# mLSTM heads in units of half the tokens, with a unit's outputs emitted behind the next unit's weights

## The chip, the core and the metric

The kernel runs on one core of one Trainium2 chip. Of the core's engines five matter here: TensorE (PE in the rows; its weight loads are PEld), VectorE (DVE), ScalarE (ACT), GpSimd (POOL) and SyncE (SP), which only issues transfers. The metric is the device time of one execution in microseconds, lower is better.

## What is computed

A two-layer bidirectional encoder on 1024 tokens of width 1024. Each layer mixes tokens with four groups of heads side by side (mLSTM, pooling windows, differential attention, grouped-query attention), then attends to a memory of 256 tokens, then runs a gated convolutional feed-forward net. The change touches the first part, the mLSTM heads above all:

```python
def mlstm_chunkwise(q, k, v, li, lf):        # per head; run forwards and, flipped, backwards
    b = cumsum(lf); a = g - b + li           # gates of a chunk
    C_loc = einsum('l,ld,le->de', exp(a - max(a)), k, v)   # what a chunk adds to the state
    ...                                      # scan over chunks: C_prev, n_prev, m_prev
    wts = exp(dlog - m_t) * einsum('td,sd->ts', q, k)      # weights inside a chunk
    num = einsum('ts,sd->td', wts, v) + exp(e - m_t) * einsum('td,de->te', q, C_prev)
    den = sum(wts) + exp(e - m_t) * einsum('td,d->t', q, n_prev)
    return num / maximum(abs(den), exp(-m_t))
```

There are 4 such heads of 64 channels in a layer, each in both directions.

## The kernel before

**Stages of a layer's mixing.** First `tok_pass` projects what is needed token by token. Then `mix` (from L1096) fills three queues of Python generators. Queue 0 holds the 15 dense projections (`qk_steps`, `ml_project`, `pool_steps`), each 48 matmuls of 512 columns (L353, L355, L357: high and low parts of both operands) into a two-bank `sc` tile. Queue 1 holds the mLSTM (`ml_gates`, then `ml_steps`). Queue 2 holds the chains behind the projections (`qk_chain`: group sums, rotation, scaling). A loop pumps them in turn: each pass hands 1 credit to queue 0, 0.6 to queue 1 and 1.0 to queue 2, and a generator says at each `yield` how many credits its step was worth. I call this the **projection stretch**. After it the attention heads run (`attend`: grouped-query first, L685 to L688, then differential, L634), and what is left in the queues is pumped behind them in small doses, along with dense work on the memory tokens (`memory_keys`, 192 matmuls of 256 columns in a layer; `memory_values`, L1381 to L1383) and the output projection.

**What sets the order.** The instructions are emitted in the order of the pumping, and a list scheduler then places them on each engine when their operands and buffers are free in its model; each engine runs its list in that order. Buffers come from pools: `work` (17 tiles named `t`), `small` (8 named `s`), `evac` (2 named `e`), and in PSUM `tp` (3 banks), `fl` (1 bank) and `sc` (2 double banks). In the built order tiles of one pool are first written in the order in which they were asked for.

**PSUM of the mLSTM.** `ml_()` gives one of the three `tp` banks while `self.wide` is set, that is, in the projection stretch, and the single `fl` bank afterwards. `memory_keys` takes the same `fl` bank once and holds it over all its 192 matmuls.

**One head** (`ml_head`): loads V, K, Q; 8 transposes of K (L947); weighted keys (DVE, L950); chunk states in two banks (L959; ACT copies L964, L965); the scan over chunks (DVE, L968). Then for each half of the tokens (I call this a **unit**): scaled queries (PE L975, DVE L977); for both directions the exponents (PE L982 and L983, ACT L988); scores (PE L996) and their product with the weights (DVE L1000); and for both directions the outputs: 8 matmuls a direction, 65 columns each (L1009 with the weights, L1012 with the state; one fewer L1012 at a sequence end), followed by the division (DVE L1017 to L1028, POOL L1029). A float32 matmul of this kind stands as two in the trace. The outputs of a unit are emitted directly behind its weights, eight matmuls between two yields of 1.5:

```python
            nc.vector.tensor_tensor(out=wt, in0=wt, in1=st.unsqueeze(1)..., op=ALU.mult)   # L1000
            yield 1.5
            for d in range(2):
                po = self.ml_()
                for c in range(4): ...                                                     # L1009, L1012
```

`ml_project` (L781) makes the mLSTM's q, k and gate projections. Its evacuation writes each half from `sc` into a tile of the two-buffer pool `evac` (L788 or L790) and stores it to DRAM by SP, from where `ml_head` loads it.

## Time and profile before

| | us |
|---|---|
| median of 3 runs | 3496.82 (3492.69 to 3504.57) |
| the profiled execution | 3500.49 |
| its span, first to last instruction | 3498.7 |
| PE busy in the span | 3302.9 (94%) |
| DVE, ACT, POOL busy | 2102.3 (60%), 1439.2 (41%), 681.8 (19%) |
| projection stretch, layer 0 and 1 | about 140 to 385 and 1890 to 2113 |
| grouped-query attention, layer 0 and 1 | about 385 to 600 and 2113 to 2330 |

In the timeline and window rows, times count from the span's start. "PEclk" is the mean granted TensorE clock of a stretch as a share of 2.4 GHz; the chip grants 2.4 GHz or 1.2 GHz (0.50), so a mean between them tells which share of the stretch ran at which. A busy PE at 0.50 is busy for twice the time.

### The profile page before, as it was taken

To read this page: it belongs to the slowest core of one execution; us is meant where nothing else is said; L and a number is where in the kernel's file an instruction comes from. 1 tells how busy PE (TensorE), PEld (TensorE's weight loads), DVE (VectorE), ACT (ScalarE), POOL (GpSimd) and SP (SyncE) were. 2 spreads that over 40 slices of the span, in tenths; PEclk is the share of its full clock that TensorE was granted. 3 is DMA by queue.
4 is the path that set the end of the run, shared out by engine and by line. 5 is a ranking of instruction groups with operands and counts; after the bars stand their busy time and mean duration, and the time that the engine had idled before them with its cause. 6 is when DMAs were issued, how large, how long until landed. Compare 5 with 4: busy or idle time off the path is not lost.

```text
span 3498.7 us, 43627 instructions
## 1 busy us (share of the span) xinstructions
PE 3302.9 (94%) x16782; PEld 2762.6 (79%) x16782; DVE 2102.3 (60%) x3266; ACT 1439.2 (41%) x2411; POOL 681.8 (19%) x484
## 2 busy tenths in 40 slices
PE   7999988999999999999999898899898999999999
PEld 7877777987777888778897777789777878887787
DVE  4445667875456777753435356778735577777432
ACT  4222556753444444431323235577535344434211
POOL 2110435842110000000112004467411100000000
PEclk9988889999999999999999888999999999999999
DMA  5343335423242222255543433344214312222654
GB/s 181 98 127 108 108 92 161 146 75 109 84 144 74 85 79 85 79 189 192 179 130 107 136 96 120 102 157 139 105 61 137 122 61 85 78 85 79 203 189 155
DMA packets 156197, 414.57 MB, mean 118 GB/s; under 512 B 31251, under 2 KB 49301, under 8 KB 155989
## 3 DMA queue, kind: packets, MB, share of 16 engines
q1 hardware_dynamic: 136372, 380.32, 33.0%
q10 hardware_dynamic: 19616, 31.46, 2.8%
q8 instruction: 132, 2.16, 0.3%
q14 instruction: 77, 0.62, 0.1%
HBM read 276.19 MB, written 128.19 MB: 116 GB/s over the span
## 4 chain that ended last, share of the span: by engine, by line
PE 77%; DVE 11%; DMA 6%; ACT 3%; issue 3%; POOL 1%; SPq 0%; ACTq 0%; DVEq 0%; POOLq 0%
PE sc L1681 15%; PE sc L353 11%; PE sc L355 11%; PE sc L357 11%; PE tp L1681 6%; DVE smax L479 2%; PE tp L537 2%; DMA raw<-w_ffn_in 1%; DVE s L542 1%; DMA yd<-s 1%; PE sc L634 1%; PE tp L1009 1%; PE tp L276 1%; PE tp L528 1%; PE tp L1012 1%
## 5 line engine op out<-in xcount | busy, mean ns | idle before, releaser
L328 ACT CAST wp<-raw 128x1024 fp32r<-128x1024 f32 (+2 forms) x174 | 165.4, 952 | 579.8 <-PE sc L355 469.0
L353 PE MATMUL sc<-h,wp 128*128 128x512 f32 x1120 | 361.1, 402 | 18.8 <-DVE e L790 9.6
L357 PE MATMUL sc<-h,wp 128*128 128x512 f32 x1120 | 359.5, 401 | 13.0 <-DVE wp L329 13.0
L355 PE MATMUL sc<-h,wp 128*128 128x512 f32 x1120 | 362.4, 402 | 0.0
L1681 PE MATMUL sc<-h,wp 128*128 128x512 f32 x1320 | 338.4, 397 | 10.7 <-DVE t L1691 7.5
L1681 PE MATMUL sc<-t,wp 128*128 128x512 f32 x1320 | 328.3, 394 | 7.3 <-DVE t L1569 4.1
L1681 PEld LDWEIGHTS sc<-h,wp 128*128 128x128 f32 x1320 | 246.8, 190 | 75.7 <-DVE t L1691 20.7
L1681 PEld LDWEIGHTS sc<-t,wp 128*128 128x128 f32 x1320 | 251.2, 191 | 61.3 <-DVE t L1569 4.7
L244 POOL TENSOR_TENSOR rb<-rb,z 128x1024 f32<-128x1024 f32 x34 | 92.2, 2712 | 901.6 <-ACT z L243 833.6
L353 PEld LDWEIGHTS sc<-h,wp 128*128 128x128 f32 x1120 | 212.8, 193 | 67.9 <-DVE e L790 10.0
L357 PEld LDWEIGHTS sc<-h,wp 128*128 128x128 f32 x1120 | 214.9, 193 | 62.6 <-DVE wp L329 15.2
L479 DVE TENSOR_REDUCE smax<-sc 128x1 f32<-128x1024 f32 x192 | 233.3, 1217 | 43.3 <-PE sc L688 24.2
L355 PEld LDWEIGHTS sc<-h,wp 128*128 128x128 f32 x1120 | 215.5, 193 | 48.8 <-issue 3.5
L482 ACT ACTIVATE h<-sc,smax 128x1024 f32<-128x1024 f32 x192 | 214.8, 1120 | 70.6 <-DVE smax L479 51.8
L1568 ACT CAST wp<-s 128x512 fp32r<-128x512 f32 x176 | 109.2, 623 | 318.6 <-PE sc L1681 296.3
L1289 DVE TENSOR_TENSOR z<-sc,z 128x1024 f32<-128x1024 f32 x64 | 78.3, 1223 | 254.5 <-PE sc L357 254.4
L353 PE MATMUL sc<-t,wp 128*128 128x512 f32 x640 | 201.1, 395 | 12.8 <-ACT wp L328 10.0
L542 DVE TENSOR_TENSOR s<-tp,s 128x512 fp32r<-128x512 f32 x256 | 172.9, 683 | 65.4 <-ACT s L541 64.2
L1681 PE MATMUL tp<-h,wp 128*128 128x512 f32 x792 | 202.0, 390 | 2.3 <-ACT wp L1568 2.3
L355 PE MATMUL sc<-t,wp 128*128 128x512 f32 x640 | 200.6, 395 | 2.4 <-DVE t L1258 2.4
L357 PE MATMUL sc<-t,wp 128*128 128x512 f32 x640 | 198.9, 392 | 0.0
L537 PE MATMUL tp<-identr,h 128*128 128x128 f32 x1024 | 183.1, 284 | 15.3 <-DVE s L542 11.7
(426 smaller groups left out, 7215.0 us busy)
## 6 DMA issues: line engine op xcount, KB each, us to landing
raw<-w_ffn_in SPq DMA_DIRECT2D x88, 512.0 KB
xd<-z SPq DMA_DIRECT2D x72, 512.0 KB
z<-xd SPq DMA_DIRECT2D x72, 512.0 KB
gd<-t SPq DMA_DIRECT2D x44, 512.0 KB
z<-gd SPq DMA_DIRECT2D x44, 512.0 KB
raw<-w_ffn_out SPq DMA_DIRECT2D x32, 512.0 KB
raw<-w_fm SPq DMA_DIRECT2D x30, 512.0 KB
raw<-w_ck SPq DMA_DIRECT2D x16, 512.0 KB
```

Of the source, the lines that this page charges most:

```text
L244: nc.gpsimd.tensor_tensor(out=st["acc"], in0=st["acc"], in1=sq, op=ALU.add)
L328: nc.scalar.copy(hi, raw)
L353: nc.tensor.matmul(o, lhsT=hi[:, k, :], rhs=xh[:, f : f + m], start=first, stop=False)
L355: nc.tensor.matmul(o, lhsT=hi[:, k, :], rhs=xl[:, f : f + m], start=False, stop=False)
L357: nc.tensor.matmul(o, lhsT=lo[:, k, :], rhs=xh[:, f : f + m], start=False, stop=last)
L479: nc.vector.tensor_reduce(out=m, in_=sc, axis=AX.X, op=ALU.max, negate=True)
L482: nc.scalar.activation(e, sc, AF.Exp, bias=m, scale=1.0, accum_out=s)
L537: nc.tensor.transpose(tp[:, (2 * j + i) * P : (2 * j + i + 1) * P], w[:, (k + j) * P : (k + j + 1) * P], self.ident)
L542: nc.vector.tensor_tensor(out=el, in0=tp, in1=eh.bitcast(F32), op=ALU.subtract)
L1289: nc.vector.tensor_tensor(out=x, in0=ps, in1=x, op=ALU.add)
L1568: nc.scalar.copy(hi, x)
L1681: mm = lambda a, b, start, stop: nc.tensor.matmul(ps, lhsT=a, rhs=b, start=start, stop=stop, skip_group_check=not first)
```

## The change

1. **Units.** `ml_head` is split into `ml_state` (loads, K transposes, states), `ml_weights` (one unit up to L1000's product) and `ml_outputs` (that unit's outputs). `ml_steps` emits a unit's outputs behind the weights of the following unit; across heads they come before the next head's state. The outputs are cut into pieces: a yield of 0.4 after each chunk's matmuls.
2. **More waiting credits.** 3 credits pass between a head's loads and its transposes, 3 more before the states.
3. **Buffers.** The scaled queries and the second direction's product go to `small` tiles instead of a `work` tile; `ml_project` evacuates into `small` instead of `evac`.
4. **Pace.** Queue 1 gets 0.7 credits a pass instead of 0.6. `qk_chain` yields between the two halves of its group sums (L276) and asks for 2 credits more in all.

```diff
@@ qk_chain
         pg = self.tp_()
+        yield 2
         for h in range(2):
             self.group_sums(pg, G, 4 * G * h, sq[h], ind, nt=4)
+            yield 1
         y = self.group_rsqrt(pg, G, dim, r[1], times=times)
-        yield 3
+        yield 1
@@ ml_project
-            t = self.e_()
+            t = self.s_()
@@ ml_state (the first part of ml_head)
             nc.sync.dma_start(out=Q[p : p + 64], in_=self.MQ[f, p0 : p0 + 64])
+        yield 3
...
-        yield 1
+        yield 3
...
+                if c == 1:
+                    yield 0.4
...
-            yield 1
+            yield 0.4
@@ ml_weights
+        WT, QS = self.t_(), self.s_()
...
-            yield 0.5
+        yield 0.4
...
-                yield 1
+            yield 0.6
...
-            yield 1.5
+        out.append((wt, QS))
+        yield 0.6
@@ ml_outputs
+                if c < 3:
+                    yield 0.4
...
-                    t = QT[:, HF : HF + 256].rearrange("p (c e) -> p c e", e=64)
+                t = self.s_()[:, :256].rearrange("p (c e) -> p c e", e=64)
...
-                yield 1.5
+            yield 0.4
@@ ml_steps
+        behind = None
         for h in range(4):
             for gen in needs[h // 2]:
                 self.until(gen)
-            yield from self.ml_head(l, h, g, HT)
+            state = []
+            if behind:
+                yield 3
+                yield from self.ml_outputs(*behind)
+                behind = None
+            yield from self.ml_state(l, h, g, state)
+            for n in range(2):
+                made = []
+                yield from self.ml_weights(l, h, n, g, state[0], made)
+                if behind:
+                    yield from self.ml_outputs(*behind)
+                behind = l, h, n, g, state[0], made[0], HT
+        yield 4
+        yield from self.ml_outputs(*behind)
@@ mix
-            self.pump(0.6, 1)
+            self.pump(0.7, 1)
```

**How it moves instructions.** Three places of layer 0; layer 1 is alike. In the names the number behind a tile is its count; lines of the changed kernel are shifted (L947 is L950 there, L959 L962, L975 L986, L982 and L983 L992 and L993, L996 L1006, L1009 and L1012 L1026 and L1029, L1000 L1010, L537 L539, L541 L543, L685 L687).

Place 1, PE where the third head begins. Before, the last outputs of the second head run into the group sums and into the third head's transposes and states:

```order
L1009 MATMUL tp_2048<-t_1685,t_1773 128x65
L1012 MATMUL tp_2048<-t_1685,t_1774 128x65
L1009 MATMUL tp_2048<-t_1685,t_1773 128x65
L276 MATMUL tp_2083<-cons,s_1951 128x4 x4
L276 MATMUL tp_2083<-cons,s_1952 128x4 x4
L947 MATMUL tp_2178<-identr,t_2172 128x64 x8
L959 MATMUL tp_2189<-t_2169,t_2177 128x65 x4
L959 MATMUL tp_2211<-t_2169,t_2177 128x65 x4
L975 MATMUL tp_2232<-t_1003,mltab 128x512
L982 MATMUL tp_2235<-t_993,mltab 128x512
```

In the changed kernel the third head's transposes stand between dense matmuls:

```order
L357 MATMUL sc_2243<-h_187,wp_2235 128x512 x2
L353 MATMUL sc_2243<-h_195,wp_2234 128x512
L950 MATMUL tp_2266<-identr,t_2204 128x64 x8
L308 MATMUL tp_2289<-identr,gy_332_2215 4x128 x4
L308 MATMUL tp_2299<-identr,gy_332_2215 4x128 x4
L353 MATMUL sc_2243<-h_195,wp_2234 128x512
L355 MATMUL sc_2243<-h_196,wp_2234 128x512 x2
```

What moved: the last outputs and the next head's start no longer form one row of small matmuls. The outputs of a unit themselves still stand as 14 or 15 of a row in both kernels.

Place 2, PE around a unit's scores. Before, the outputs of the unit whose scores these are follow at once:

```order
L982 MATMUL tp_1976<-t_993,mltab 128x512
L983 MATMUL tp_1976<-mltab,identr 128x512
L996 MATMUL tp_2000<-t_1690,t_1688 128x128 x4
L1009 MATMUL tp_2018<-t_1685,t_1773 128x65
L1012 MATMUL tp_2018<-t_1685,t_1774 128x65
```

In the changed kernel the outputs behind the scores read the weights of the unit before (t_2351, not the product of tp_2442):

```order
L355 MATMUL sc_2536<-h_188,wp_2531 128x512 x2
L357 MATMUL sc_2536<-h_187,wp_2532 128x512 x2
L353 MATMUL sc_2536<-h_195,wp_2531 128x512 x2
L687 MATMUL sc_2711<-t_1621,t_1629 128x512
L1006 MATMUL tp_2442<-t_2206,t_2204 128x128 x4
L1026 MATMUL tp_2472<-t_2201,t_2351 128x65 x2
L1029 MATMUL tp_2472<-t_2201,s_2352 128x65
```

What moved: a unit's outputs no longer follow its own scores.

Place 3, ACT in the grouped-query attention, where the memory keys end. L328 makes the high part of a weight, L1365 to L1370 (L1331 to L1336 before) evacuate the memory keys' `fl` bank, L541 (L543) makes attention operands. Before, attention's casts stand between those of the memory keys:

```order
L541 CAST s_3056<-tp_3051 128x512
L328 CAST wp_3699<-raw_3698 128x1024
L1331 COPY z_2847<-fl_2850 128x256
L1336 ACTIVATE e_3446<-fl_2850 128x256
L541 CAST s_3074<-tp_3069 128x512
L541 CAST s_3109<-tp_3104 128x512
L328 CAST wp_3961<-raw_3960 128x1024
```

In the changed kernel the last head's states, in `fl`, and its scaled queries come first:

```order
L328 CAST wp_5012<-raw_5011 128x1024
L1365 COPY z_2775<-fl_2777 128x256
L1370 ACTIVATE e_4718<-fl_2777 128x256
L969 COPY t_2656<-fl_2900 64x260
L970 COPY t_2656<-fl_2900 64x3x65
L969 COPY t_2656<-fl_2952 64x195
L970 COPY t_2656<-fl_2952 64x4x65
L543 CAST s_3001<-tp_2996 128x512
```

On PE at the same place the last 125 memory-key matmuls stand in a row and then this:

```order
L357 MATMUL fl_2777<-h_2740,wp_4582 128x256
L950 MATMUL fl_2803<-identr,t_2659 128x64 x8
L962 MATMUL fl_2900<-t_2656,t_2802 128x65 x4
L962 MATMUL fl_2952<-t_2656,t_2802 128x65 x4
L986 MATMUL fl_2993<-t_994,mltab 128x512
L529 MATMUL tp_2976<-s_3001,t_1627 128x256
```

What moved: before, only the fourth head's last unit (and one direction of the unit before it) lies in the `fl` bank, behind the memory keys; now the fourth head's states and both its units do, and ACT makes no attention operand between the cast of the keys' fourth weight and the end of that head's states. From the end of the memory keys to the start of `memory_values` (the next dense matmuls of this stretch) PE's list transposes attention weights of 13 blocks of 128 queries before (from the 10th to the 23rd) and of 21 now (from the 4th to the 25th).

## Rows read from the trace of the kernel before

**Rows 1.** Cores: span and mean granted TensorE clock.

```profile
core 0: 3498.7 us, clock 0.957
```

**Rows 2.** Windows: stretch, length, busy time (instructions) of PE, PEld, DVE, ACT, POOL; PEclk; DMA.

```profile
140.00:385.00 245.00, 233.34 (x1059) 185.28 (x1057) 126.67 (x245) 70.92 (x139) 36.77 (x32) 0.87 0.39 120
...
465.00:535.00 70.00, 60.65 (x342) 51.29 (x341) 54.76 (x104) 41.40 (x80) 30.60 (x21) 0.87 0.29 91
...
605.00:745.00 140.00, 135.71 (x1038) 127.25 (x1037) 126.73 (x212) 102.45 (x181) 106.56 (x84) 1.00 0.36 123
...
1890.00:2113.00 223.00, 210.05 (x957) 165.71 (x955) 114.39 (x228) 66.97 (x132) 31.07 (x28) 0.87 0.37 113
```

**Rows 3.** Waits of PE in layer 0's projection stretch: total us, times, longest.

```profile
PE sc L353 <- DVE e L790: 4.3, 1, 4.3
PE tp L947 <- DMA t<-mkd: 1.8, 1, 1.8
```

**Rows 4.** The same of layer 1.

```profile
PE sc L353 <- DVE e L790: 5.4, 1, 5.4
PE tp L947 <- DMA t<-mkd: 3.1, 1, 3.1
```

**Rows 5.** Line L1000: who waited for it (us, times), both layers.

```profile
  PE tp L1009: 5.1, 4
```

**Rows 6.** Timeline of DVE, layer 0: start, length, instruction, idle before and its releaser.

```profile
225.19 0.69 DVE L790 SCALAR_TENSOR_TENSOR e<-sc,rb 128x512 f32<-128x512 f32 x1 [10.11 <-DMA mkd<-e]
```

**Rows 7.** Timeline of PE, layer 0, two runs of small matmuls.

```profile
272.86 0.44 PE L1009 MATMUL tp<-t,t 128*128 128x65 f32 x2
273.23 0.43 PE L1012 MATMUL tp<-t,t 64*128 64x65 f32 x2
...
302.54 0.69 PE L1009 MATMUL tp<-t,t 128*128 128x65 f32 x2
303.15 0.69 PE L1012 MATMUL tp<-t,t 64*128 64x65 f32 x2
...
312.63 1.11 PE L947 MATMUL tp<-identr,t 64*128 64x64 f32 x8
315.43 3.65 PE L959 MATMUL tp<-t,t 128*128 128x65 f32 x16 [1.69 <-DVE ry L216]
```

**Rows 8.** Windows of the longest stretch at the lower clock in each layer.

```profile
301.10:321.60 20.50, 18.82 (x76) 16.21 (x76) 6.89 (x28) 2.48 (x9) 0.72 (x1) 0.50 0.30 72
2041.90:2062.40 20.50, 18.82 (x77) 15.89 (x76) 7.40 (x29) 3.62 (x11) 0.72 (x1) 0.50 0.25 60
```

**Rows 9.** Timeline of ACT in the attention of layer 0 and of layer 1.

```profile
447.50 0.59 ACT L541 CAST s<-tp 128x512 fp32r<-128x512 f32 x1 [10.52 <-DMA yd<-s]
...
2183.61 0.59 ACT L541 CAST s<-tp 128x512 fp32r<-128x512 f32 x1 [8.73 <-DMA yd<-s]
```

**Rows 10.** Waits of PE from 385 to 605, and from 2113 to 2335.

```profile
PE tp L527 <- DVE s L542: 11.1, 4, 8.0
...
PE tp L527 <- DVE s L542: 9.1, 3, 6.2
```

**Rows 11.** Windows, L537's transposes alone (PE, PEld; eight for 128 queries).

```profile
465.00:535.00 70.00, 19.95 (x107) 14.25 (x106) 0.87 0.29 91
```

**Rows 12.** Groups by line from 385 to 605: count, busy us, mean ns, idle before.

```profile
L329 POOL TENSOR_TENSOR wp<-raw,wp 128x1024 fp32r<-128x1024 f32 x14 | 33.4, 2391 | 23.1 <-ACT wp L328 23.1
L328 ACT CAST wp<-raw 128x1024 fp32r<-128x1024 f32 x14 | 14.6, 1053 | 16.3 <-issue 6.5 <-PE fl L355 3.9 <-PE fl L1382 2.8
...
L964 ACT COPY t<-tp 64x195 f32<-64x195 f32 x1 | 0.3, 302 | 0.0
```

**Rows 13.** Timeline of PE: two neighbouring matmuls of the memory keys.

```profile
432.63 0.28 PE L353 MATMUL fl<-h,wp 128*128 128x256 f32 x1
432.74 0.28 PE L355 MATMUL fl<-h,wp 128*128 128x256 f32 x1
```

**Rows 14.** Line L950: duration min/median/max in ns.

```profile
L950 DVE TENSOR_TENSOR t<-tp,mtok x16: 679/682/692, 160.1 to 2118.6; 128x512 f32<-128x512 f32 x16
```

More of the change, by code (lines that the diff above doesn't have):

```diff
@@ L927, in ml_gates, with ml_state @@
         out.append((pairs, tok, fb))
-    def ml_head(self, l, h, g, HT):
+    def ml_state(self, l, h, g, out):
         nc = self.nc
-        (mt, si), tok, fb = g[0]
+        _, tok, fb = g[0]
         f, p0 = h // 2, (h % 2) * 64
-        hf = lambda: self.t_()
-        vc = hf()
+        vc = self.t_()
         V = vc[:, : 8 * 65].rearrange("p (c e) -> p c e", e=65)
@@ L938, in ml_head @@
         nc.gpsimd.memset(V[:, :, 64:65], 1.0)
-        K = hf()[:64]
+        K = self.t_()[:64]
         nc.sync.dma_start(out=K, in_=self.MK[f, p0 : p0 + 64])
-        Q = hf()
+        Q = self.t_()
         for p in (0, 64):
             nc.sync.dma_start(out=Q[p : p + 64], in_=self.MQ[f, p0 : p0 + 64])
-        KW = hf().rearrange("p (c d e) -> p c d e", d=2, e=64)
+        yield 3
+        KW = self.t_().rearrange("p (c d e) -> p c d e", d=2, e=64)
         pk = self.ml_()
@@ new lines, in ml_state, with ml_weights @@
+        out.append((V, C, K, Q))
+    def ml_weights(self, l, h, n, g, state, out):
+        nc = self.nc
+        (mt, si), tok, _ = g[0]
+        _, _, K, Q = state
+        sl = slice(n * HF, (n + 1) * HF)
+        WT, QS = self.t_(), self.s_()
+        pi = self.ml_()
+        nc.tensor.matmul(pi, lhsT=self.ml_sel(h)[:100], rhs=si[:100, sl], start=True, stop=True)
+        nc.vector.tensor_tensor(out=QS, in0=Q[:, sl], in1=pi, op=ALU.mult)
+        yield 0.4
+        for d in range(2):
+            pm = self.ml_()
+            one = self.mltab[:100, h * P + 64 * d : h * P + 64 * d + 1].to_broadcast([100, P])
+            nc.tensor.matmul(pm, lhsT=one, rhs=mt[:100, sl], start=True, stop=False)
+            nc.tensor.matmul(
+                pm, lhsT=self.identr, rhs=self.mltab[:, (4 + d) * P : (5 + d) * P].unsqueeze(1).to_broadcast([P, 4, P]),
+                start=False, stop=True,
+            )
+            for c in range(4):
+                nc.scalar.activation(
+                    WT[:, d * HF + c * P : d * HF + (c + 1) * P], pm[:, c * P : (c + 1) * P], AF.Exp,
+                    bias=tok[:, 0, d, 4 * n + c, h : h + 1], scale=-1.0,
+                )
+            yield 0.6
+        st = self.ml_()
+        for c in range(4):
+            o = (4 * n + c) * P
+            nc.tensor.matmul(
+                st[:, c * P : (c + 1) * P], lhsT=K[:, o : o + P], rhs=Q[:64, o : o + P], start=True, stop=True
+            )
+        wt = WT.rearrange("p (d n) -> p d n", d=2)
+        nc.vector.tensor_tensor(out=wt, in0=wt, in1=st.unsqueeze(1).to_broadcast([P, 2, HF]), op=ALU.mult)
+        out.append((wt, QS))
+        yield 0.6
@@ new lines, in ml_outputs @@
+    def ml_outputs(self, l, h, n, g, state, made, HT):
+        nc = self.nc
+        tok = g[0][1]
+        V, C, _, _ = state
+        wt, QS = made
+        for d in range(2):
+            po = self.ml_()
+            for c in range(4):
+                cc = 4 * n + c
+                prev = cc - 1 if d == 0 else cc + 1
+                inter = 0 <= prev < 8
+                out = po[:, c * 65 : (c + 1) * 65]
+                nc.tensor.matmul(out, lhsT=wt[:, d, c * P : (c + 1) * P], rhs=V[:, cc, :], start=True, stop=not inter)
+                if inter:
+                    q = slice(64 * d, 64 * d + 64)
+                    nc.tensor.matmul(
+                        out, lhsT=QS[q, c * P : (c + 1) * P], rhs=C[q, prev if d == 0 else 7 - prev, :], start=False, stop=True
+                    )
+                if c < 3:
+                    yield 0.4
+            ov = po[:, :260].rearrange("p (c e) -> p c e", e=65)
+            den = self.tiny(4, tag="mden", bufs=3)
+            nc.vector.tensor_reduce(
+                out=den, in_=ov[:, :, 64:65], axis=AX.X, op=ALU.max, apply_absolute_value=True
+            )
+            nc.vector.tensor_tensor(out=den, in0=den, in1=tok[:, 2, d, 4 * n : 4 * n + 4, h], op=ALU.max)
+            nc.vector.reciprocal(den, den)
+            db = den.unsqueeze(2).to_broadcast([P, 4, 64])
+            dst = HT[n][:, :, h, :]
+            if d == 0:
+                nc.vector.tensor_tensor(out=dst, in0=ov[:, :, 0:64], in1=db, op=ALU.mult)
+            else:
+                t = self.s_()[:, :256].rearrange("p (c e) -> p c e", e=64)
+                nc.vector.tensor_tensor(out=t, in0=ov[:, :, 0:64], in1=db, op=ALU.mult)
+                nc.gpsimd.tensor_tensor(out=dst, in0=dst, in1=t, op=ALU.add)
+            yield 0.4
```

53 lines of the change are left out of this document (removed).

## The prediction

> **What bounds the kernel now.** I read the span and the clock first. The core runs 3498.7 us at a mean granted clock of 0.957 [rows 1], and PE is busy for most of every stretch, so a change gains only where PE idles or is granted 1.2 GHz, and moves nothing by shifting work between other engines. The windows by stage say where that is. In the projection stretch PE is busy 233.3 of 245 us in layer 0 and 210.1 of 223 in layer 1, and its clock is 0.87 in both [rows 2]. In the first part of the attention, once the memory keys are through, it is busy 60.7 of 70 us, again at 0.87, while in the differential attention it is busy 135.7 of 140 at 1.00 [rows 2]. So there are three pools to gain from or lose to: PE's waits in the projection stretch, its slow clock there, and the poorly filled stretch of attention. The waits by releaser, the timeline around the longest slow stretches, and the attention's stalls then give the terms below. All sums are over both layers.
>
> **The evacuation tile.** PE waits 4.3 and 5.4 us for L790, the evacuation of an mLSTM projection [rows 3, 4], and L790 itself had stood 10.1 us for a DMA: its tile, one of two in `evac`, still held data on the way to DRAM [rows 6]. With `small` the tile comes from eight buffers, and in the built order those it takes had been given up long before by group sums or earlier stores. What stays is the evacuation itself, 0.69 us [rows 6]. Of 9.7 us I take 9 as gained. The bounds are 9.7 and nothing: nothing if the unit's scaled queries, which now hold a `small` buffer from one unit to the next, make the projections wait in their place.
>
> **The outputs behind the next weights.** PE waits 5.1 us for L1000, the product that a unit's outputs need [rows 5]. Place 2 of the order shows these outputs now behind another unit's scores, so the product has that unit's weights as its cover. If that cover is gone, as at a head's last unit, the 4 credits at the end and the 3 before a new head take its place. The K loads cost PE 1.8 and 3.1 us [rows 3, 4]; the 3 credits between load and transposes let dense matmuls run there. Together 10.0 us; I take 9, with 10 and 0 as bounds. The finer cuts of the outputs have no price: place 1 says that they still stand as 14 or 15 in a row.
>
> **The clock in the projection stretch.** 0.87 between two levels of 1.00 and 0.50 means 26% of the time at 1.2 GHz: 64 us of 245 and 58 of 223, 122 us in all [rows 2]. What it costs is read from one pair of output matmuls: L1009 to L1012 takes 0.37 us before the clock falls (272.86 to 273.23) and 0.61 after (302.54 to 303.15) [rows 7]. So 40% of the slow time is lost, 49 us. The two longest slow stretches, 20.5 us each [rows 8], are where a run of outputs, group sums, transposes and chunk states follows without one dense matmul (312.63 and 315.43 [rows 7]; place 1). They cost 0.4 x 41 = 16 us. In the changed order that run is broken up, but each unit's outputs remain a run. I take 14 of the 49 as gained. The bounds are 0 (the clock falls after every run of outputs anyway) and 25 (half of it).
>
> **What moves into the attention.** The fourth head's states and one more unit leave the projection stretch in each layer: 8 transposes and 16 state matmuls (1.1 and 3.7 us at the slow clock [rows 7], so 2.9 us at the fast), five 512-column and eight score matmuls (2.3 us, an estimate from the same spacing), and 8 output matmuls (16 in the trace, 2.9 us by the 0.37 us for two [rows 7]): about 8 us. It is no new work. It gains as far as it falls where PE idles, and PE idles 9.4 us in 70 there [rows 2]. I take half, 4 us a layer, 8 in all; bounds 0 and 16.
>
> **The stall in the attention.** In both layers ACT stops 10.5 and 8.7 us for a `small` tile whose store to DRAM hasn't landed [rows 9], and PE loses 8.0 and 6.2 us to it through the operand that DVE then makes late [rows 10]. In the changed order the buffer of that store is asked for again only after more steps, and attention is at another place when the store goes out. I take 11 of the 14.2 us as gained, bounds 14.2 and 0.
>
> **The memory keys and the fourth head in one bank.** Here the change adds a wait. The fourth head's first transposes wait for `fl`, which the memory keys hold to their end; its scaled queries therefore ask late for a `small` buffer, and all attention operands asked for later queue behind it (place 3). PE then runs 125 key matmuls in a row, about five weights of 24. A weight takes PE 24 x 0.12 = 2.9 us [rows 13], but ACT and POOL need 1.05 + 2.39 = 3.4 us to make it [rows 12]: 0.6 us idle each, 3 us. Then the head's first steps stand on PE with nothing between: the two products of L950 at 0.68 us [rows 14] and two pairs of copies at 0.30 a copy [rows 12], with the last evacuation 3.4 us or a bit more. That is 6.4 us a layer, 13 in all; bounds 4 (the weights lie ready) and 20 (each handover costs twice that).
>
> **Attention without dense matmuls.** From the keys' end to the memory values, attention goes through 21 blocks of queries instead of 13. In the stretch where it does so now, 107 transposes are 13.4 blocks [rows 11]; there 9.4 us are idle and 26% of 70 us run slow, at 40% lost another 7.3 [rows 2]. That is 1.25 us a block, 10 us for 8 more blocks, 20 in all. Since the last head's matmuls stand in between I take 18. The lower bound is 5, a quarter of it, and the upper 40, twice the price.
>
> The Trainium skill, TensorE: Matmul & The Clock Gate, section "A second HAM failure mode: psum-queue depth-cycling", speaks against this part: a PE that pauses briefly between groups while it goes through PSUM banks swings between its two clocks. By that rule every step of the fourth head in the single bank would cost clock, and this term would lie at its upper bound, 40, and the sum at +2. The stretch shown has steps of that kind and runs at 0.87 [rows 2], so the trace agrees in kind; how much more a whole head brings no row shows.
>
> **The sum.** -9 - 9 - 14 - 8 - 11 + 13 + 18 = -20 us. The sum is made against the profiled execution, whose own time is 3500.5 us, 1.8 above its span; the median of the runs is 3.7 us lower, 3496.8. The forecast is 3496.8 - 20 = 3477 us, 0.6% faster.
>
> **The rivals.** *The clock gives more.* With 25 instead of 14 for the clock, and the attention without dense matmuls at 5, the sum is -9 - 9 - 25 - 8 - 11 + 13 + 5 = -44: 3453 us. For it: the two 20.5 us stretches [rows 8] have a plain cause that place 1 removes. Against it: the runs of outputs, which come before the other falls, are as long as before.
>
> *The waits only change their name.* The clock falls after each run of outputs as now (0), and the `small` pool, shared by scaled queries, squares, evacuations and pooling, gives back half of the evacuation's gain (5): -5 - 9 - 0 - 8 - 11 + 13 + 18 = -2: 3495 us. The change then doesn't do what it says, as the uncut runs of place 1 suggest.
>
> *Attention stops and isn't made up.* Place 3 leaves ACT, DVE and POOL without attention work while five or six weights go through at 3.4 us each, some 21 us a layer. If attention later runs at DVE's pace, as the differential part nearly does (126.7 of 140 us, with PE at 135.7 [rows 2]), that time comes back as 42 us at the end of attention, in which the other terms (-51 + 31) still hold: +22, 3519 us. It decides from about 30 of the 42 lost, where the time passes 3507. Against it: PE has less than 5 us in 140 free there [rows 2], so PE's work, which doesn't grow, sets that stretch's end more than DVE's.
>
> **How the numbers follow.** Forecast 0.45, more from the clock 0.15, no net change 0.22, slower 0.18. A measurement of this kernel can't tell less than 0.3%, some 10 us, from no change; the first two cases lie beyond that, so faster 0.60, same 0.22, slower 0.18. The likeliest case's own terms scatter some 12 us either way, 3465 to 3489. The range reaches to 3449, a little under the clock's case, and to 3512, into the slower one: it leaves out about 1 in 10 on each side.
>
> **What would show it.** PE's wait for L790's line is gone from both projection stretches, and with it the wait of that evacuation for a DMA. No wait of the outputs for the weights' product is left there. PEclk in the projection stretch is 0.90 to 0.92, and no stretch of 20 us at 0.50 is left around the third head's start. In the first part of the attention, ACT's 10 us stop for a store is gone, and instead there is a stretch of some 17 us with memory-key matmuls alone and a gap of 3 to 5 us in all behind it; PE's idle time from there to the memory values is larger than the 9.4 us in 70 seen now. The forecast is wrong if the clock in the projection stretch stays at 0.87 (then 3495), or if the attention lasts more than 15 us longer in each layer than the projection stretch got shorter (then above 3507).

## The result, and the profile after

The changed kernel takes 3550.9 us (median of 4 runs, 3548.1 to 3555.1) where the kernel before took 3495.6 beside it: a ratio of 1.0154, with a 95% interval of 1.0136 to 1.0172. It is 55 us **slower**; forecast was 20 us faster. The span of the profiled run grew by 50.5 us, from 3498.7 [rows 1] to:

```profile
core 0: 3549.2 us, clock 0.951
```

The windows by stage show where. A row is a stretch, its length, the busy time of PE, PEld, DVE, ACT and POOL, then PEclk. The kernel before, layer 0: from the first head's K transposes to the first memory key, to the last key, to the first memory value, to the last value, to the end of the mixing; the last row is that whole stretch.

```profile
159.00:412.70 253.70, 238.70 (x1091) 187.80 (x1091) 142.95 (x290) 84.42 (x169) 42.48 (x38) 0.86 0.35 110
412.70:464.10 51.40, 43.45 (x322) 41.67 (x321) 22.22 (x47) 25.78 (x49) 26.29 (x16) 0.90 0.45 128
464.10:537.50 73.40, 63.87 (x358) 53.87 (x357) 58.08 (x109) 42.93 (x81) 30.88 (x21) 0.85 0.30 94
537.50:605.20 67.70, 58.58 (x411) 52.61 (x411) 44.64 (x70) 42.06 (x76) 37.01 (x26) 0.96 0.47 153
605.20:771.40 166.20, 158.13 (x1205) 147.17 (x1204) 140.72 (x244) 112.04 (x199) 113.65 (x88) 1.00 0.31 107
159.00:771.40 612.40, 562.72 (x3378) 483.12 (x3378) 408.61 (x758) 307.23 (x572) 250.32 (x189) 0.91 0.36 114
```

The same stages of the changed kernel:

```profile
162.20:402.90 240.70, 221.58 (x994) 173.59 (x994) 124.90 (x257) 78.11 (x148) 36.88 (x33) 0.85 0.35 110
402.90:454.00 51.10, 35.54 (x252) 33.43 (x251) 15.54 (x28) 19.00 (x36) 24.87 (x16) 0.90 0.38 124
454.00:578.60 124.60, 102.60 (x614) 85.33 (x613) 88.41 (x180) 72.27 (x141) 42.81 (x32) 0.88 0.25 80
578.60:633.40 54.80, 46.29 (x350) 42.81 (x349) 37.33 (x59) 35.34 (x62) 36.22 (x24) 0.99 0.60 202
633.40:799.70 166.30, 158.48 (x1177) 146.55 (x1176) 135.63 (x236) 105.66 (x190) 109.58 (x85) 0.98 0.29 95
162.20:799.70 637.50, 564.49 (x3378) 481.71 (x3378) 401.82 (x758) 310.39 (x574) 250.37 (x189) 0.91 0.34 109
```

The projection stretch got 13 us shorter. The memory keys take as long as before, though PE runs 70 matmuls fewer beside them, and from the last key to the first memory value it is 124.6 us instead of 73.4. Over the whole stretch PE runs the same 3378 matmuls in each layer and is busy 1.8 us longer in layer 0 and 9.4 in layer 1: 11 us more. It idles 73.0 us instead of 49.7 (length less PE busy), in layer 1 76.5 instead of 50.7: 49 us more. Together these are the 60 us by which the two layers' mixing is longer; everything outside it is 10 us shorter. By the mean clock to three places (0.906 and 0.904, before 0.911 and 0.926) 44 us more run at 1.2 GHz; at the prediction's 40% that would be 18 us, where PE's busy time grew by 11. A busy PE doesn't take twice the time for everything at 1.2 GHz: two output matmuls took 0.61 us instead of 0.37 [rows 7].

Two new waits stand out. PE's waits in the projection stretch, layer 0 and layer 1, where before the evacuation and a short wait for K stood [rows 3, 4]:

```profile
PE tp L950 <- DMA t<-mkd: 12.2, 1, 12.2
PE tp L314 <- DVE rows L310: 4.5, 2, 4.0
...
PE tp L950 <- DMA t<-mkd: 11.5, 1, 11.5
PE tp L314 <- DVE rows L310: 5.2, 1, 5.2
```

No wait for the evacuation and none of the outputs for L1010's product is left. But the second head's transposes now stand on PE long before K is there. SP's queue in the changed kernel (a row is an issue: start, how long it held SP):

```profile
203.84 5.43 SPq L663 DMA_DIRECT2D t<-gvd  x1
220.27 0.39 SPq L1336 DMA_DIRECT2D z<-memT  x1
220.76 0.45 SPq L327 DMA_DIRECT2D raw<-w_fm  x1
221.41 0.48 SPq L428 DMA_DIRECT2D gqd<-t  x1
232.60 0.57 SPq L669 DMA_DIRECT2D t<-gqd  x1
233.22 1.08 SPq L939 DMA_DIRECT2D t<-mvd  x1
234.35 4.29 SPq L942 DMA_DIRECT2D t<-mkd  x1
```

The head's loads stand behind the load of the memory tokens, the store of the grouped heads' queries and the load that waits for that store. In the kernel before the load of K went out at 226.92 and PE took it at 239.12; here it goes out at 234.35, and PE, which wanted it at 235.09, takes it at 247.31.

The second new wait is in the memory keys. PE waits before each of the last five of the eight weights for ACT's evacuation of the keys, and on ACT that evacuation stands behind the cast of a weight, which itself waits for PE to give back a buffer. First PE's waits, then ACT (the last row is a cast that waited for its weight's load, and with it the PE row at 444.16):

```profile
422.36 0.39 PE L353 MATMUL fl<-h,wp 128*128 128x256 f32 x1 [1.63 <-ACT z L1367]
427.12 0.39 PE L353 MATMUL fl<-h,wp 128*128 128x256 f32 x1 [1.63 <-ACT e L1370]
...
444.16 0.58 PE L353 MATMUL fl<-h,wp 128*128 128x256 f32 x1 [9.16 <-ACT e L1370]
```

```profile
420.70 1.04 ACT L328 CAST wp<-raw 128x1024 fp32r<-128x1024 f32 x1 [2.87 <-PE fl L355]
421.65 0.37 ACT L1365 COPY z<-fl 128x256 f32<-128x256 f32 x1
421.92 0.39 ACT L1367 ACTIVATE z<-fl 128x256 f32<-128x256 f32 x1
...
442.50 1.04 ACT L328 CAST wp<-raw 128x1024 fp32r<-128x1024 f32 x1 [10.68 <-DMA raw<-w_ck]
```

Meanwhile attention stands still. DVE has nothing to do until the fourth head's states:

```profile
420.18 1.23 DVE L481 TENSOR_REDUCE smax<-sc 128x1 f32<-128x1024 f32 x1 [2.15 <-PE sc L690]
456.66 1.29 DVE L953 TENSOR_TENSOR t<-fl,mtok 128x512 f32<-128x512 f32 x2 [35.26 <-PE fl L950]
```

The clock shows the same trade. The two stretches of 20.5 us [rows 8] are gone, and others stand instead: right behind the wait for K in layer 0, at the end of layer 0's projections, and at the end of layer 1's.

```profile
239.00:252.00 13.00, 4.70 (x21) 3.61 (x22) 2.89 (x5) 1.15 (x2) 0.00 (x0) 0.50 0.45 84
372.00:388.50 16.50, 15.92 (x54) 13.35 (x55) 9.01 (x24) 6.32 (x7) 7.90 (x9) 0.50 0.48 177
2130.00:2153.50 23.50, 21.40 (x70) 16.61 (x71) 15.20 (x37) 11.59 (x16) 10.15 (x11) 0.50 0.34 129
```

### The profile page after: what moved, and what is told of

Its sections match the earlier page's. It is cut to its first block, busy times and chain, and to the rows that moved or that the text cites. A ratio compares the mean times of both kernels' runs of the same rounds, so it can differ in the third digit from the quotient of the medians.

```text
span 3549.2 us, 43624 instructions
## 1 busy us (share of the span) xinstructions
PE 3312.9 (93%) x16782; PEld 2768.4 (78%) x16782; DVE 2086.5 (59%) x3266; ACT 1445.4 (41%) x2415; POOL 682.1 (19%) x484
## 5 line engine op out<-in xcount | busy, mean ns | idle before, releaser
L328 ACT CAST wp<-raw 128x1024 fp32r<-128x1024 f32 (+2 forms) x174 | 165.3, 950 | 593.6 <-PE sc L355 462.2
L544 DVE TENSOR_TENSOR s<-tp,s 128x512 fp32r<-128x512 f32 x256 | 173.3, 682 | 50.6 <-ACT s L543 49.2
L539 PE MATMUL tp<-identr,h 128*128 128x128 f32 x1024 | 180.0, 282 | 12.0 <-DVE s L544 6.7
```

Source lines behind the costliest of these rows:

```text
L328: nc.scalar.copy(hi, raw)
L539: nc.tensor.transpose(tp[:, (2 * j + i) * P : (2 * j + i + 1) * P], w[:, (k + j) * P : (k + j + 1) * P], self.ident)
L544: nc.vector.tensor_tensor(out=el, in0=tp, in1=eh.bitcast(F32), op=ALU.subtract)
```

## The experiments

The experiments test four explanations of the loss: **D**, the credits added to `qk_chain` make K's load late; **S**, what stands ahead of that load on SP does; **Q**, the stopped attention costs; **H**, the fourth head in the `fl` bank delays the memory values, and attention without dense matmuls is the cost. The ratio is always to the kernel before, run on the same chip (medians 3495.6 to 3505.5).

| run | ratio (95% interval) | PE idle, mixing, us | at 1.2 GHz, us |
|---|---|---|---|
| kernel before | 1 | 100.4 | 198 |
| changed kernel | 1.0154 (1.0136 to 1.0172) | 149.5 | 242 |
| e1 changed, own pool | 1.0119 (1.0102 to 1.0137) | 131.7 | 277 |
| e2 changed, old `qk_chain` | 1.0194 (1.0177 to 1.0211) | 156.9 | 297 |
| e3 before, evacuation alone | 1.0000 (0.9987 to 1.0013) | 107.0 | 229 |
| e4 changed, e1 and e2 | 1.0255 (1.0240 to 1.0270) | 165.5 | 379 |
| e5 changed, outputs direct | 1.0109 (1.0084 to 1.0135) | 111.6 | 236 |
| e6 changed, loads on ACT | 1.0068 (1.0047 to 1.0088) | 121.7 | 215 |
| e7 before, e3 and loads on ACT | **0.9936** (0.9913 to 0.9958) | 91.3 | 174 |
| e8 e7, pace 0.8 | 1.0112 (1.0090 to 1.0134) | 110.2 | 263 |
| e9 e6, own pool | 1.0117 (1.0086 to 1.0149) | 140.9 | 277 |
| e10 e6, outputs direct, `work` tile | 1.0067 (1.0042 to 1.0093) | 112.4 | 259 |
| e11 e7, put behind | 1.0145 (1.0105 to 1.0186) | 139.6 | 276 |
| e12 e7, pace 0.7 | 1.0105 (1.0074 to 1.0136) | 124.6 | 259 |
| e13 e6, fourth head in `tp` | 1.0034 (1.0021 to 1.0047) | 106.5 | 253 |
| e14 e7, fourth head in `tp` | 1.0085 (1.0062 to 1.0107) | 125.0 | 225 |
| e15 e7, units only | 1.0068 (1.0047 to 1.0089) | 111.2 | 239 |

Idle is the time in which PE runs nothing, both layers, from the first head's transposes to the end of the mixing; the last column is twice (1 less the mean granted clock) times that stretch's length. A least-squares line through the 17 kernels, length = 1080 + 0.72 x idle + 0.34 x time at 1.2 GHz, misses none by more than 14 us, so these two columns say where the time goes. As idle time is a part of the length, the line is bookkeeping and names no cause. Both columns are of the one profiled execution; that of e3 was 11 us above its median, that of e10 13 above and that of e8 11 below.

**The wait for the evacuation, and the load of K.** e3 and e7 edit the kernel before:

```diff
-            t = self.e_()
+            t = self.s_()
...
-        nc.sync.dma_start(out=K, in_=self.MK[f, p0 : p0 + 64])
+        nc.scalar.dma_start(out=K, in_=self.MK[f, p0 : p0 + 64])
...
```

The first pair, `ml_project`'s evacuation, is e3. The second, with the same edit for V and Q, comes to it in e7.

> The kernel before with one line of the change: the evacuation of the mLSTM projections takes a `small` tile instead of an `evac` tile. By the prediction's first term PE's waits of 4.3 and 5.4 us for that evacuation go, and nothing else moves much: 9 us less, 3486 (0.9974). Rival: the eight `small` tiles are asked for in turn with squares and pooling, and what is gained comes back as other waits: within 3 us of 3495.6.

Measured 1.0000: nothing gained. PE's waits in e3, layer 0 and layer 1:

```profile
PE tp L947 <- DMA t<-mkd: 13.8, 1, 13.8
...
PE tp L947 <- DMA t<-mkd: 14.5, 1, 14.5
```

The 4.3 us for the evacuation are gone and 13.8 us for K stand instead of 1.8. K's load goes out at 226.61, in the kernel before at 226.92, and PE takes K at 241.44 and 239.12: the load is no earlier, but PE comes to it 9.6 us sooner. That is the evacuation's wait and more: 143 dense matmuls of 512 columns stand between the first and the second head's transposes instead of 170, so the scheduler's list has changed too. The prediction's first two terms are one chain here, not two: what PE no longer waits for at the evacuation it waits for at K.

> The kernel before with two edits: the projections' evacuation in `small` (as in the run with that line alone, where PE waited 13.8 us for the second head's K instead of 4.3 us for the evacuation and 1.8 us for K), and the loads of a head's V, K and Q issued by ScalarE. If the evacuation's 9.7 us were only handed on to the load of K on SP, both are gone now: 10 to 15 us less than before, 3481 to 3487 (0.9957 to 0.9971). If the clock takes them, within 4 us of before.

Measured 0.9936, 3478 us, 22 less than before by the ratio, more than the 10 to 15 expected: the only kernel here that beats both. PE waits 1.5 and 5.2 us for K and not for the evacuation. The loads alone, without the evacuation's tile, weren't tried on the kernel before, so the 22 us aren't shared out between the two edits.

e6 moves the same loads in the changed kernel:

> The changed kernel with the loads of a head's V, K and Q issued by ScalarE instead of SyncE, so that they no longer stand behind the load of the memory tokens, the query's store and its load on SP. Theory S (what stands ahead on SP makes L950 wait): PE's waits of 12.2 and 11.5 us for the load of K fall to 3 us or less, and the time falls by 15 to 24 us, to 3527 to 3536. Rival C (PE's time is given back as a slower granted clock or as waits of the same projections elsewhere): the waits go, the time stays within 8 us of 3551.

Measured 1.0068, 28 us less than the changed kernel and more than expected. The load is issued in 0.46 us, and PE's waits for it are 5.8 and 3.7 us, not quite the 3 or less that were expected:

```profile
227.30 0.46 ACTq L942 DMA_DIRECT2D t<-mkd  x1
```

```profile
233.50 1.09 PE L950 MATMUL tp<-identr,t 64*128 64x64 f32 x8 [5.85 <-DMA t<-mkd]
```

Idle time fell by 28 us, and only 14 of them are these waits. Another 13 went in the memory keys, where the waits for one late weight in each layer, 9.2 and 10.8 us, are 3.0 and 3.7 here, and 8 with the wait of L314; 8 us came back during the memory values. Why the keys' weights came earlier isn't shown. 27 us less run at 1.2 GHz, but PE's busy time in the mixing is only 5 us shorter. S holds for the wait for K, and the clock didn't take back what was won.

e2 puts the yields of `qk_chain` back (`yield 3` for `yield 2`, `1, 1`, `1`):

> The changed kernel with the yields of `qk_chain` as in the kernel before (1, 3 instead of 1, 2, 1, 1, 1). Theory D (the 2 credits more hold the query's store of the grouped heads back by some 10 us, and the second head's load of K stands behind the load of that store on SP; PE waits 12.2 and 11.5 us for it): the wait of L950's transposes on the load of K falls to 4 us or less in each layer, and the time falls by 10 to 20 us, to 3531 to 3541. Rival S (the load is late because of what stands before it on SP, the load of the memory tokens that waits 11 us for a buffer): the wait stays at 10 us or more, the time within 8 us of 3551.

Measured 1.0194, slower still and outside both expectations, with PE waiting longer for K in both layers:

```profile
PE tp L948 <- DMA t<-mkd: 20.0, 1, 20.0
...
PE tp L948 <- DMA t<-mkd: 19.0, 1, 19.0
```

D falls. The query's store goes out earlier there (211.44 instead of 221.41), but in that order other loads stand ahead of K's, two of which hold SP for 5.8 and 6.6 us, and K's goes out at 238.76:

```profile
224.97 5.80 SPq L327 DMA_DIRECT2D raw<-w_fm  x1
...
232.08 6.64 SPq L937 DMA_DIRECT2D t<-mvd  x1
238.76 8.68 SPq L940 DMA_DIRECT2D t<-mkd  x1
```

**The stopped attention.** e1 gives the scaled queries tiles that no attention operand waits behind, and takes two from `small` for it:

```diff
-        self.ps = pool("small", 8)
+        self.ps = pool("small", 6)
+        self.pqs = pool("scaled", 2)
...
-        WT, QS = self.t_(), self.s_()
+        WT, QS = self.t_(), self.tile(self.pqs, [P, HF], F32, "qs")
```

> The changed kernel, but the scaled queries take their tile from a pool of their own (2 tiles; `small` keeps 6 of its 8), so that no attention operand queues behind the fourth head's scaled queries any more. Changed kernel: 1.0154 of before (3551 us). Theory Q (the queue for `small` stops the attention during the memory keys, 420 to 463 us in layer 0, and PE idles 20 us a layer more than before): attention rows stand between the key matmuls again, ACT's and DVE's 43 us without attention work in that stretch are gone, PE's idle time between 398 and 578 us falls from 37.7 us to about 20, and the time falls by 25 to 40 us, to 3511 to 3526. Rival L (the fourth head and the memory keys share the one `fl` bank, and the whole tail of the head stands late, whoever waits): attention runs in the stretch, but PE's idle time only moves behind it; the time stays above 3540.

Measured 1.0119: attention does run beside the keys, and little comes of it: 12 us by the ratios, 7 by the medians. But it stops there again in another way. An attention operand now waits for a `small` tile whose store hasn't landed, the stall of [rows 9] at greater length, and PE waits with it (10.1 us in layer 1):

```profile
PE tp L530 <- ACT s L544: 9.2, 1, 9.2
...
ACT s L544 <- DMA yd<-s: 12.0, 1, 12.0
```

Behind the keys PE now waits for nearly every step of the fourth head, and the stretch to the memory values runs at 0.77, as a timeline of PE and the window show:

```profile
461.96 0.50 PE L993 MATMUL fl<-t,mltab 100*128 100x512 f32 x1 [1.23 <-ACT t L999]
464.11 2.07 PE L1007 MATMUL fl<-t,t 64*128 64x128 f32 x8 [1.23 <-ACT t L999]
```

```profile
449.80:567.50 117.70, 94.69 (x498) 77.13 (x496) 69.28 (x153) 54.34 (x109) 31.95 (x24) 0.77 0.21 69
```

e9 does the same with the loads on ACT:

> The changed kernel with the head's loads issued by ScalarE and the scaled queries in a pool of their own (2 tiles beside 6 of `small`): attention no longer stops during the memory keys and no load of K is late. If the stopped attention is what is left of the loss (the changed kernel with the loads alone stood at 1.0068 of before), the time comes down to 1.000 or less (3500). If the fourth head in the single `fl` bank is what costs, stopped attention or not (with the own pool alone PE waited 1.2 us at each of some nine steps of that head, and the granted clock between keys and memory values was 0.77), the gain is 8 us or less: 1.0045 to 1.007 (3515 to 3523).

Measured 1.0117 against 1.0068: 17 us slower, outside both expectations. The keys' stretch, from its start to the first memory value, takes 187 us instead of 170, with the clock at 0.79 instead of 0.89 behind the keys. The stall for a `small` tile is there too, and longest here (12.3 us of PE in layer 1):

```profile
PE tp L531 <- DVE s L545: 17.0, 1, 17.0
...
DVE s L545 <- DMA yd<-s: 19.5, 1, 19.5
```

So e1 and e9 trade one stop for another, and `small` has two tiles fewer in both. That running attention beside the keys isn't worth its price isn't shown by them, and Q stays open: no run has the scaled queries' own pool beside all 8 `small` tiles.

e4 joins e1 and e2:

> The changed kernel with both: a pool of their own for the scaled queries, and the yields of `qk_chain` as before. If Q and D are both right and act in different stretches, the gains add: 35 to 60 us less than the changed kernel, 3491 to 3516. If one of the two only moves the other's wait, the time is that of the better one alone.

Measured 1.0255, the slowest of all, slower than either edit alone and outside both expectations. PE waits 15.0 and 16.3 us for K, and 379 us run at 1.2 GHz.

**The fourth head in the `fl` bank.** e5 emits a unit's outputs directly, e10 besides with a `work` tile and the loads on ACT:

```diff
...
                 yield from self.ml_weights(l, h, n, g, state[0], made)
-                if behind:
-                    yield from self.ml_outputs(*behind)
-                behind = l, h, n, g, state[0], made[0], HT
+                yield from self.ml_outputs(l, h, n, g, state[0], made[0], HT)
...
```

> The changed kernel, but a unit's outputs are emitted directly behind its own weights again (the 3 and 4 credits that stood before the outputs put behind go with them); buffers, the other credits, queue 1's pace of 0.7 and `qk_chain` stay as changed. In the built order only the fourth head's last unit is then left for the `fl` bank, mLSTM's finishing transposes stand behind 16 to 19 score tiles of attention instead of 28 to 32, and the memory values begin behind 24 instead of 37; attention still stands still during the memory keys (192 key matmuls in a row). Theory H (the fourth head in the `fl` bank sets when the memory values begin, and attention without dense matmuls until then is the main cost): the stretch from the last key to the first memory value falls from 125 us to about 70 in each layer, and the time to 3505 to 3525. Rival Q (the blocked attention is the main cost): the time stays within 10 us of 3551.

Measured 1.0109, 3537 us, 12 above the times expected by H and below those of the rival. The stretch from keys to memory values fell to 76 us as H says, but the one behind the values grew:

```profile
447.80:523.90 76.10, 59.27 (x330) 49.74 (x329) 53.65 (x114) 38.96 (x75) 27.05 (x18) 0.83 0.35 116
...
579.70:787.60 207.90, 192.69 (x1414) 173.00 (x1413) 174.71 (x299) 141.72 (x255) 135.98 (x108) 1.00 0.32 107
```

166.3 us there in the changed kernel, 207.9 here. My reading, which no run tests by itself: dense work that runs earlier is missing later, and the attention has its length. PE doesn't wait for K at all in this order, which by e6 alone is worth much of the gain.

> The changed kernel without its units put behind: outputs directly behind their own weights, scaled queries and second product in a `work` tile, the head's loads issued by ScalarE; the finer yields, the 3 credits, the pace of 0.7, `qk_chain` and the evacuation in `small` stay. Only the fourth head's last unit and a half is left for the `fl` bank, as in the kernel before, and attention runs during the memory keys. If the fourth head's place is what costs, the time is near that of the kernel before with the same two repairs (0.9936): 3475 to 3490. If the finer yields, the credits or the pace cost, it stays above 3505.

Measured 1.0067, the same as e6. Two things differ between them, though: the outputs come directly, and the scaled queries take a `work` tile for each unit, which in e15 below costs 44 us on e7. So the equal ratios don't show that putting outputs behind makes no difference, and which of the tile, the finer yields, the credits and the pace keeps e10 from e7's time isn't told apart.

e13 and e14 finish the mLSTM in the three `tp` banks:

```diff
+        self.flush(1)
         self.wide = False
```

> The changed kernel with the loads issued by ScalarE (1.0068) and, beyond that, the rest of the mLSTM emitted before the pool of three `tp` banks is given up, so that nothing of the fourth head is left for the single `fl` bank; the memory keys then have that bank for themselves, attention runs beside them, and the memory values begin behind 25 score tiles instead of 37. If the shared `fl` bank is what is left of the loss, the time falls by 20 to 40 us, to 3483 to 3503. If it is only the place of the work (a head's last matmuls with no dense ones beside them run slow wherever they stand), the time stays within 10 us of 3523.

Measured 1.0034: 15 us less than e6 by the medians, 12 by the ratios, between the two expectations. With nothing of the head in `fl`, idle falls by 15 us, and 38 us more run at 1.2 GHz in longer projection stretches. The memory values begin 92 us after the first key instead of 170, and the stretch behind them is 197 us instead of 157.

> The kernel before with its two repairs (evacuation in `small`, loads issued by ScalarE: 0.9936) and the same edit: the fourth head's last unit and a half in the `tp` banks. The pace of 0.8, which also empties the bank, lost 61 us, but by moving all heads. If the bank matters, 5 to 15 us less than 3478: 3463 to 3473. If the slow outputs beside attention cost as much as the bank, 3475 to 3490.

Measured 1.0085, 48 us slower than e7 and outside both expectations: the same edit that helps the changed kernel hurts the kernel before. So moving the head out of the bank is worth some 12 us in the changed kernel, and H as a rule falls: in e5, e8, e13 and e14 the memory values begin earlier, counted from the first key, and the stretch behind them is 32 to 61 us longer than in the kernel each was made from.

**The parts alone, on e7.** e8 and e12 change queue 1's pace alone (0.8, 0.7 instead of 0.6):

> The same two edits on the kernel before, and queue 1's pace 0.8 instead of 0.6, so that all four heads end in the projection stretch and none is left for the `fl` bank; memory values then begin behind 29 score tiles instead of 32. Theory H expects the stretch from the last key to the first memory value shorter than the 73 us of before (about 60), and the time 15 to 30 us less than before, 3466 to 3481. Rival: the fourth head's outputs in the projection stretch slow its clock (0.86 there now) by as much as they save: within 5 us of the kernel before with the two edits alone.

> The kernel before with the two repairs and, of the change, queue 1's pace of 0.7 instead of 0.6 alone. At 0.8 the same kernel lost 61 us: its projection stretches were 21 and 27 us longer, and what follows them no shorter. If the loss grows with the share of the fourth head that is pulled into the projection stretch, 0.7 loses about half: 3500 to 3515. If the loss at 0.8 came only from the last outputs without any projection left beside them, 0.7 is within 8 us of 3478.

Measured 1.0112 and 1.0105, both outside what was expected of them. The loss doesn't grow with the pace: 0.7 costs all of it. In both, layer 0's projection stretch is over 20 us longer and its clock lower than e7's 0.87, and what follows it to the end of the mixing is 7 and 9 us longer as well (the row is e12's):

```profile
160.30:430.70 270.40, 246.84 (x1089) 192.87 (x1088) 140.00 (x287) 87.24 (x175) 42.39 (x38) 0.82 0.33 105
```

e11 puts the outputs behind, with all yields of before, and takes its two `work` tiles (weights, scaled queries) for each unit instead of each head. e15 is its control, with the same units and tiles but the outputs direct:

> The kernel before with the two repairs (evacuation in `small`, loads issued by ScalarE: 0.9936) and of the change the one idea alone: a unit's outputs are emitted behind the next unit's weights, with the yields, the pace and `qk_chain` of before and the scaled queries in a `work` tile per unit. In the built order the fourth head then falls to the `fl` bank as in the changed kernel, and the memory values begin behind 37 score tiles. If that place is what costs, the time goes up by 25 to 45 us to 3503 to 3523. If the putting behind by itself is harmless or good, it stays at 3470 to 3485.

> Control for the run in which only the putting behind was added to the kernel before with its two repairs (1.0145 against 0.9936): the same split into units with a `work` tile per unit for the scaled queries, but the outputs directly behind their own weights. If the putting behind is the cause of those 75 us, this kernel is near 0.9936: 3470 to 3490. If the tile per unit (two of the 17 `work` tiles more in turn) is the cause, it is near 3550; a time between shares it out.

Measured 1.0145, above both expectations, and 1.0068. Of the 75 us that e11 loses, the control, which emits its work in e7's order and only asks for tiles more often, loses 44; its projection stretch is 257.4 us at 0.81 instead of 243.9 at 0.87. The putting behind adds some 31 us. Most of it goes with PE's wait for K, which comes back although ACT issues the load (5.9 and 7.6 us in the control):

```profile
PE tp L947 <- DMA t<-mkd: 14.8, 1, 14.8
...
PE tp L947 <- DMA t<-mkd: 20.2, 1, 20.2
```

## Why the prediction was wrong

The step that failed is counting a wait as gained without following what PE meets next and what feeds that. The two terms on waits (-9 and -9) left K's load out or took it for covered; it stood in SP's queue, and PE waited 18.8 us longer for it. The term on the memory keys and the fourth head (+13) missed the evacuations behind the weights' casts and the late weights there; that idle time came to 45 us.

Both signs that the prediction named for its failure came. The clock of the projection stretch is 0.85 and 0.84 in the two layers. From the first key to the end of the mixing it takes 38 and 51 us longer, while the projection stretch got 13 and 15 us shorter. By the prediction's terms:

- **The evacuation tile** (-9): the wait went as forecast, and nothing was gained. The step that failed is "Of 9.7 us I take 9 as gained." without asking what PE reaches next: the transposes of the second head, whose K hasn't landed. In e3, with this edit alone, PE waits 28.3 us for K instead of 4.9.
- **The outputs behind the next weights** (-9): the 5.1 us for L1000's product went. The wait for K was to go too, because 3 credits stand between load and transposes; it grew from 4.9 to 23.7 us. The step took the credits for time: they order the emission, while the load waits in SP's queue behind a store and its reload. I had put no cost on SP's queue. With the loads on ACT (e6) 14 of the 23.7 us go, in a kernel that is 28 us faster in all.
- **The clock in the projection stretch** (-14): the two stretches of 20.5 us went and others came. 146.8 us run at 1.2 GHz there instead of 140.0: +3. That a long run of small matmuls makes those stretches fits these two, which went when the run was broken up; as a sum it failed.
- **What moves into the attention** (-8): mis-sized. 97 matmuls left layer 0's projection stretch, 17 us of busy PE, twice the 8, and the attention had no idle room for them: PE idles more there than before.
- **The stall in the attention** (-11): gone at its place, and replaced. Behind the keys PE now waits 10.6 us for L544 in layer 0, 5.9 of it while ACT stands for the reload of the mLSTM's own output (z<-yd).
- **The memory keys and the fourth head in one bank** (+13): in part right in kind, and too small. I had 0.6 us a weight from POOL and ACT; it is 1.6, since on ACT the cast of a weight stands before the evacuation that PE waits for. In each layer one weight's load came late besides (waits of 9.2 and 10.8 us), in layer 0 issued behind 11 us of attention's loads on SP: 20 us for which the prediction had no term. Idle in the keys is 31.9 us in both layers, and the head's first steps add 1.6 + 1.4 + 0.8 + 0.8 + 0.4 + 1.6 = 6.6 a layer: 45 in all, 25 without the late weights.
- **Attention without dense matmuls** (+18): some 24. From the last key to the first value idle grew by 24 us in both layers, 13 of them those steps; 32 us more at the lower clock add 13. By the rule in the Trainium skill, TensorE: Matmul & The Clock Gate, "A second HAM failure mode: psum-queue depth-cycling", the prediction said, it would lie at its upper bound, 40; this stretch did run below full clock, at 0.88 in both layers, but the rows' price was nearer.
- **The rival "attention stops and isn't made up"** had the right sign; whether its mechanism holds stays open. DVE stood idle for 35 us in one piece, more than the 21 foreseen. By the 33rd score tile, the first of the differential part, layer 0 has made it up: 209 us after the first tile (211 in the kernel before; in layer 1 212 and 200). By the last of the 96 it hasn't: 412 and 411 us after the first instead of 395 and 383. In e1 and e9, where attention runs beside the keys, it is longer still (424 and 418, 426 and 420), but with the stall for a `small` tile.

With the new wait of L314 (+10) and small waits of before that went (-9), the terms as measured are -10 - 5 + 19 + 10 - 9 + 3 - 14 + 45 + 24 = +63, for 60 in the mixing; the moved work has no term of its own, since what it cost stands in the others.

**What stays open.** Moving the loads (28 us) and the head out of `fl` (12 us) bring the changed kernel to 1.0034. It still stands 34 us above e7. The pace alone, the tiles per unit alone and the putting behind each lose 30 to 60 us on e7, while the changed kernel has the same pace and the putting behind, takes a `work` and a `small` tile for each unit, and, repaired, loses less than some of them alone. So the parts don't add, and why an order of the same work has 60 or 100 us at 1.2 GHz in a layer's projection stretch isn't settled by these runs. Nor is what the stopped attention costs.

## What to carry to other kernels

Before a wait counts as gained, look for what the engine reaches next and when that is ready, in the queue that brings it too: here, with 9.7 us of waits taken away, PE came sooner to a load that stood behind a store on SP and nothing was gained; with the loads moved to another queue as well, 22 us were. A credit or a place in a list is not time; a load's lead is what the issuing queue leaves of it. Where a scheduler sets the order, test a change against a control that alters only the buffer requests, for that alone cost 44 us here.

## What the runs showed of the hardware

The issue of one load held SP for very different times: 0.45 us for a weight (220.76), 4.29 us for K (8.68 in e2), 0.46 for K on ACT's queue in e6. From issue to PE's use it took 247.31 - 234.35 = 13.0 us on SP and 233.50 - 227.30 = 6.2 on ACT. ACT's queue isn't free of this: in e11 the issue of Q's two loads held it for 6.89 us (237.58), and K was used 9.5 us after its issue.

A wait can cost more than its length: behind PE's 12.2 us for K the granted clock stayed at 1.2 GHz until 252, nearly 5 us after PE ran again. By the prediction's 40% that is some 2 us more, an estimate.
